# A decoder trunk on one core: where the low parts of the leading weights are made at the hand-over between two products

## The chip, the cores and the metric

The kernel runs on one core of one Trainium2 chip. What is measured is the device time of one execution in microseconds (us); lower is better. Engines are named as the profile names them: PE is TensorE, with its weight loads as PEld; DVE is VectorE, ACT is ScalarE, POOL is GpSimd, SP is SyncE, which here only issues transfers.

## The reference

A decoder trunk of two layers on a sequence of 512 positions, model width 1024, all in float32. Each layer has a token mixer and a dense SwiGLU network, each between two RMS norms:

```python
normed = rms_norm(h, mix_norm_pre[layer])
mixed = retention_mixer(...) if layer < N_A_LAYERS else nsa_mixer(..., shared)
h = h + rms_norm(mixed, mix_norm_post[layer])
normed = rms_norm(h, ffn_norm_pre[layer])
h = h + rms_norm(swiglu_ffn(normed, ffn_w_in[layer], ffn_w_out[layer]), ffn_norm_post[layer])
```

The first mixer is a retention, the second a sparse attention over keys and values that are computed once between the layers (`nsa_shared_kv`). `rms_norm` multiplies by the reciprocal root of the mean square over the 1024 features and by a gain. So every product is followed by two norms in a row: one of the product, which is added to the stream `h`, and one of `h`, whose result is the input of the next product.

## The kernel before

Every float32 product is made of three products of the short type float32r. Each operand is split into a high part (a ScalarE copy that rounds, L208 and L237) and a low part (the difference of the operand and its high part, L209 and L238), and `mm3` (L243 to L245) adds high by high, high by low and low by high. Weights stream in by chunks of 128x1024 (512 KB): `raw_weights` (L225) issues the transfer from SP into one of three raw buffers, ScalarE makes the high part, another engine the low part; a raw buffer is free for the next transfer when both have read it. Kept parts live in an arena `R` of 60 slots of 128x512, from which `weights(keep=True)` takes two pairs.

The change lies in `out_stage`, which ends a mixer or a network. It computes an output product row-wise, positions on the partitions: four blocks `b` of 128 positions, two halves `c` of 512 features, one PSUM bank for each. The last five chunks of half 1 are kept (`kept`), so that blocks 0 and 1 can be finished first, and blocks 2 and 3 after them. In the third of the three stages spoken of here, a sixth chunk (`defer`) is treated so as well. While TensorE computes blocks 2 and 3, `norm(..., 0)` works on blocks 0 and 1: a reciprocal root by three Newton steps on 128x2 numbers on VectorE (`rsqrt`, L266 to L273), the addition to `h` (L352, VectorE), the squares of `h` with their sum (L353, ScalarE), a second reciprocal root (L354 and `rsqrt`), and the scaled rows (L356 on ScalarE for the one block, L357 on VectorE for the other). Then `turn(t, p, kp, ...)` transposes two slabs of 128 features of a pair `p` of blocks on TensorE (L366, four transposes), and ScalarE and VectorE split them into the high and low parts of the next product's input (L369, L370). `lead` fetches and splits the first six weight chunks of the next product, "the leading weights", and `prods(j, k, cs)` multiplies chunk `j` by slab `k` for half of the positions, 256 columns. Three chunks are multiplied as slabs appear, three after all slabs. Then `norm(..., 1)` and `turn(..., 1, ...)` do the same for blocks 2 and 3, whose products `rest` makes later.

Order. PE and DVE follow the written order inside `manual_schedule`; ACT, POOL and SP instructions there are placed by the framework's scheduler. `pool_lo` is true inside this part, so the low parts of the leading weights go to GpSimd. There are three such stages: the retention's output (leads the network of layer 0), that network's output (leads the shared keys and values, and also copies the turned slabs, L376), and the attention's output (leads the network of layer 1). The fourth call of `out_stage` returns early and has no lead.

Of the kernel before, what the change touches and what calls it, by code (L numbers as in the profile page):

```python
# [10 lines left out]
F32 = mybir.dt.float32  # L11
# [3 lines left out]
OP = mybir.AluOpType  # L15
# [19 lines left out]
NR, NF = 60, 27  # L35
RAW, SPL = 3, 2
TAIL = 10

G_MIXPRE0, G_MIXPOST0, G_FFNPRE0, G_FFNPOST0, G_KV, G_MIXPRE1, G_MIXPOST1, G_FFNPRE1, G_FFNPOST1 = range(9)

# [127 lines left out]
class Trunk:  # L168
    def __init__(self, ctx, tc, a):
        self.tc, self.nc, self.a = tc, tc.nc, a  # L170
        pool = lambda name, **k: ctx.enter_context(tc.tile_pool(name=name, bufs=1, **k))
        self.cst = pool("cst")
        self.wp = pool("wp")
        arena = pool("arena")
        self.R = Arena(arena, NR, F32R, "r")
        self.F = Arena(arena, NF, F32, "f")
        self.banks = pool("ps", space=bass.MemoryType.PSUM).tile([P, 8, S], F32, name="banks")
        self.dram = pool("dram", space=bass.MemoryType.DRAM)
        self.n = 0
        self.pool_lo = False  # L180
        nc = self.nc
        self.ones = self.cst.tile([P, P], F32, name="ones")
        nc.gpsimd.memset(self.ones, 1.0)
        self.ident = self.cst.tile([P, P], F32, name="ident")
        nc.gpsimd.dma_start(self.ident, a["ident"])
        self.gains = self.cst.tile([P, 9, KT], F32, name="gains")
        nc.sync.dma_start(self.gains, a["gains"])
# [40 lines left out]
    def weights(self, src, off, row, n, keep=False):  # L228
        raw = self.raw_weights(src, off, row, n)
        if keep:  # L230
            w = Pair(self.R.take(2), self.R.take(2))
            hi, lo = w.hi.ap, w.lo.ap
        else:
            hi = self.wp.tile([P, 1024], F32R, name=self.nm("whi"), tag="whi", bufs=SPL)
            lo = self.wp.tile([P, 1024], F32R, name=self.nm("wlo"), tag="wlo", bufs=SPL)
            w = Pair(hi, lo)
        self.nc.scalar.activation(hi[:, :n], raw[:, :n], AF.Copy)  # L237
        (self.nc.gpsimd if self.pool_lo else self.nc.vector).tensor_tensor(lo[:, :n], raw[:, :n], hi[:, :n].bitcast(F32), op=OP.subtract)  # L238
        return w

    def mm3(self, out, shi, slo, mhi, mlo, start, stop):
# [98 lines left out]
        for x in st["x"]:  # L340
            x.free()

    def norm(self, h, t, sq, pre, p):

        nc = self.nc
        bs = slice(2 * p, 2 * p + 2)
# [3 lines left out]
        for i in range(2):  # L350
            b = 2 * p + i
            nc.vector.scalar_tensor_tensor(h[b].ap, t[b].ap, r[:, i:i + 1], h[b].ap, op0=OP.mult, op1=OP.add)  # L352
            nc.scalar.activation(t[b].ap, h[b].ap, AF.Square, accum_out=s2[:, i:i + 1])  # L353
        nc.vector.tensor_scalar(m2, s2, 1.0 / D, EPS, op0=OP.mult, op1=OP.add)  # L354
        r2 = self.rsqrt(m2, 2, True)
        nc.scalar.activation(t[2 * p].ap, h[2 * p].ap, AF.Copy, scale=r2[:, 0:1])  # L356
# [21 lines left out]
    def out_stage(self, x, src, nk, gpost, gpre, get_h, lead, banks, late=None, begun=None, keep=None):  # L378
# [15 lines left out]
        def chunk(c, i, keep=False):  # L394
            return self.weights(src, c * P * nk * S + i * S, nk * S, 2 * S, keep)

        def mm(c, i, w, blocks):
            for kk in range(2):
                k, ws = i + kk, slice(kk * S, (kk + 1) * S)
                for b in blocks:  # L400
                    bs = slice(b * P, (b + 1) * P)
                    self.mm3(bank[c][b], x[k].hi[:, bs], x[k].lo[:, bs], w.hi[:, ws], w.lo[:, ws], k == 0, k == nk - 1)
# [52 lines left out]
        E = mybir.EngineType  # L455
        st = self.state()
        st["n"] = []
        self.pool_lo = True
        with self.tc.manual_schedule(engines={E.PE, E.DVE}):
            for b in range(2):  # L460
                for i in kept:
                    mm(1, i, kept[i], (b,))
                evac(1, b)
            self.norm(h, t, sq, pre[0], 0)
            if begun:
                mm(0, begun, defer, (2, 3))
                defer.free()
                for b in (2, 3):
                    evac(0, b)
                pre[1] = early(1)  # L470
            for i in kept:
                mm(1, i, kept[i], (2, 3))
                kept[i].free()
                free(i)
            for b in (2, 3):
                evac(1, b)
            row.free()
            order, ws, prods = lead(st, A + B[:2])
            for kp in range(KT // 2 + 1):
                if kp < KT // 2:  # L480
                    self.turn(t, 0, kp, bank[1][kp % 2], gpre, st, keep is not None)
                if kp:
                    for k in (2 * kp - 2, 2 * kp - 1):
                        for j in range(3):
                            prods(j, k, HALVES[0])
            for b in range(2):
                t[b].free()
            for j in range(3, len(order)):
                for k in range(KT):
                    prods(j, k, HALVES[0])  # L490
            self.norm(h, t, sq, pre[1], 1)
            for kp in range(KT // 2):
                self.turn(t, 1, kp, bank[1][2 + kp % 2], gpre, st, keep is not None)
            for b in (2, 3):
                t[b].free()
        if keep is not None:
            for b in range(NB):
                nc.scalar.dma_start(keep[b], h[b].ap)
                h[b].free()
        self.pool_lo = False  # L500

        def rest(j0):
            j = order.index(j0)
# [7 lines left out]

    def lead(self, x, src, tiles, banks, base=0):

        ws = [self.chunk(src, j, KT, 0, base=base, keep=True) for j in tiles]

        def prods(j, k, cs):
            ks = slice(k * P, (k + 1) * P)
            self.mm3(self.banks[:, banks[j], cs], ws[j].hi[:, ks], ws[j].lo[:, ks], x[k].hi[:, cs], x[k].lo[:, cs],
                     k == 0, k == KT - 1)
        return tiles, ws, prods  # L520

    def ffn_lead(self, l):
        def go(st, banks):
# [1099 lines left out]
```

## Time and profile before

| | us |
|---|---|
| median of 3 runs (lowest, highest) | 1513.77 (1512.81, 1514.18) |
| the profiled execution | 1516.28 |
| span of its instructions | 1514.5 |

The profile is of one execution. Its span runs from the first to the last instruction; the execution's own time is 1.8 us longer. A row of a timeline gives the start in the span, the duration, the engine, the line, the operation, what it writes and reads, and in brackets how long the engine stood idle before it and what ended that. A row ending in "x2" holds two instructions back to back. TensorE's products overlap: a 128x512 product is listed with 0.39 us, though the next one starts 0.227 us later. "PEclk" is the clock that TensorE was granted, as a share of 2.4 GHz; 0.50 is its other level, 1.2 GHz.

### The profile page before, as it was taken

The page shows a single profiled execution, that of the slowest core. Times are in us where ns is not written, and L with a number is a line of the kernel's source. Part 1 is how long each engine was busy: PE and PEld are TensorE (multiplying, and loading weights), DVE is VectorE, ACT ScalarE, POOL GpSimd, SP SyncE. Part 2 cuts the span into 40 slices and gives each one's busy share as a digit, 9 for nine tenths or more (in the row PEclk, how much of TensorE's full clock was granted, in tenths as well). Part 3 has the DMA queues.
Part 4 walks back from the last instruction along what each step waited for, and adds up shares of the span by engine and source line. Part 5 has one row for each costly group of instructions (what it writes and reads, how often), then busy time and mean ns, then how long its engine had stood idle before and what let it go on. Part 6 is the DMA issues. An engine that isn't in the chain of part 4 may idle for free.

```text
span 1514.5 us, 18688 instructions
## 1 busy us (share of the span) xinstructions
PE 1473.5 (97%) x7294; PEld 1242.8 (82%) x7294; DVE 741.1 (49%) x1297; ACT 599.3 (40%) x1048; POOL 294.2 (19%) x387
## 2 busy tenths in 40 slices
PE   8999999999989999999998999999989999999997
PEld 6888888888788888888877978888879888888886
DVE  7456464735553333332345646888755333333234
ACT  5333343333332222221335337889744222222131
POOL 2022121211300000000030737877440000000000
PEclk9999999999989999999998999999998999999999
DMA  5222232325312344332342341221240232332231
GB/s 205 83 78 84 78 97 77 98 80 174 125 57 84 122 130 137 114 104 97 111 148 89 112 159 61 87 84 50 89 134 30 69 97 95 110 95 95 97 123 56
DMA packets 47833, 151.87 MB, mean 100 GB/s; under 512 B 5744, under 2 KB 6384, under 8 KB 47744
## 3 DMA queue, kind: packets, MB, share of 16 engines
q1 hardware_dynamic: 46560, 147.47, 30.3%
q10 hardware_dynamic: 1152, 3.15, 0.5%
q8 instruction: 57, 0.93, 0.2%
q14 instruction: 32, 0.26, 0.1%
q0 software_dynamic: 32, 0.07, 0.0%
HBM read 141.22 MB, written 9.44 MB: 99 GB/s over the span
## 4 chain that ended last, share of the span: by engine, by line
PE 91%; DVE 5%; ACT 2%; issue 1%; DMA 1%; POOL 0%; SPq 0%; DVEq 0%; ACTq 0%
PE banks L244 27%; PE banks L243 27%; PE banks L245 27%; PE banks L1470 2%; PE banks L1492 1%; PE banks L1404 1%; PE banks L1405 1%; PE banks L1491 1%; PE banks L983 1%; DVE t L270 1%; PE banks L366 1%; DVE u L271 1%; DVE y L266 0%; PE banks L1302 0%; DVE f L352 0%
## 5 line engine op out<-in xcount | busy, mean ns | idle before, releaser
L237 ACT ACTIVATE whi<-raw 128x1024 fp32r<-128x1024 f32 x165 | 174.7, 1059 | 514.9 <-PE banks L244 330.8
L243 PE MATMUL banks<-r,whi 128*128 128x512 f32 x920 | 361.4, 393 | 0.0
L245 PE MATMUL banks<-r,wlo 128*128 128x512 f32 x920 | 360.1, 391 | 0.0
L244 PE MATMUL banks<-r,whi 128*128 128x512 f32 x920 | 359.2, 390 | 0.0
L238 DVE TENSOR_TENSOR wlo<-raw,whi 128x1024 fp32r<-128x1024 f32 x165 | 206.0, 1249 | 296.3 <-ACT whi L237 290.2
L243 PE MATMUL banks<-r 128*128 128x256 f32 (+2 forms) x600 | 197.5, 338 | 7.7 <-ACT r L208 5.8
L244 PE MATMUL banks<-r 128*128 128x256 f32 (+2 forms) x600 | 201.2, 338 | 3.1 <-DVE r L370 2.5
L245 PEld LDWEIGHTS banks<-r,wlo 128*128 128x128 f32 x920 | 172.4, 187 | 37.5 <-DVE f L648 0.7
L244 PE MATMUL banks<-wlo,r 128*128 128x512 f32 x520 | 202.9, 390 | 0.0
L245 PE MATMUL banks<-whi,r 128*128 128x512 f32 x520 | 202.6, 390 | 0.0
L243 PEld LDWEIGHTS banks<-r,whi 128*128 128x128 f32 x920 | 172.5, 188 | 36.2 <-issue 1.6
L244 PEld LDWEIGHTS banks<-r,whi 128*128 128x128 f32 x920 | 172.5, 187 | 35.2 <-issue 0.5
L245 PE MATMUL banks<-r 128*128 128x256 f32 (+2 forms) x600 | 198.3, 334 | 0.0
L243 PE MATMUL banks<-whi,r 128*128 128x512 f32 x520 | 178.5, 390 | 0.0
L243 PEld LDWEIGHTS banks<-r 128*128 128x128 f32 x600 | 115.5, 196 | 20.4 <-ACT r L208 5.8
L244 PEld LDWEIGHTS banks<-r 128*128 128x128 f32 x600 | 117.6, 196 | 16.3 <-DVE r L370 5.5
L238 POOL TENSOR_TENSOR r<-raw,r 128x1024 fp32r<-128x1024 f32 x18 | 43.9, 2457 | 434.3 <-ACT r L237 421.7
L245 PEld LDWEIGHTS banks<-r 128*128 128x128 f32 x600 | 117.6, 196 | 10.0 <-DVE r L209 0.2
L245 PEld LDWEIGHTS banks<-whi,r 128*128 128x128 f32 x520 | 97.6, 188 | 20.3 <-issue 0.2
L244 PEld LDWEIGHTS banks<-wlo,r 128*128 128x128 f32 x520 | 97.7, 188 | 20.2 <-issue 0.2
L243 PEld LDWEIGHTS banks<-whi,r 128*128 128x128 f32 x520 | 97.7, 188 | 19.8
L545 DVE TENSOR_TENSOR f<-banks,f 128x512 f32<-128x512 f32 x44 | 30.4, 691 | 137.7 <-PE banks L245 133.6
(175 smaller groups left out, 1721.9 us busy)
## 6 DMA issues: line engine op xcount, KB each, us to landing
raw<-in_ffn_w_in_dram SPq DMA_DIRECT2D x88, 512.0 KB, 3.5
raw<-in_ffn_w_out_dram SPq DMA_DIRECT2D x44, 512.0 KB, 3.3
raw<-in_ret_w_g_dram SPq DMA_DIRECT2D x16, 512.0 KB, 3.5
raw<-in_ret_w_v_dram SPq DMA_DIRECT2D x16, 512.0 KB, 3.7
raw<-in_ret_w_out_dram SPq DMA_DIRECT2D x16, 512.0 KB, 3.8
f<-rows SPq DMA_DIRECT2D x32, 256.0 KB, 2.6
raw<-in_ret_w_qk_dram SPq DMA_DIRECT2D x12, 512.0 KB, 3.5
rows<-f SPq DMA_DIRECT2D x16, 320.0 KB, 4.4
```

Of the source, the lines that this page charges most:

```text
L237: self.nc.scalar.activation(hi[:, :n], raw[:, :n], AF.Copy)
L238: (self.nc.gpsimd if self.pool_lo else self.nc.vector).tensor_tensor(lo[:, :n], raw[:, :n], hi[:, :n].bitcast(F32), op=OP.subtract)
L243: t.matmul(out, shi, mhi, start=start, stop=False)
L244: t.matmul(out, shi, mlo, start=False, stop=False)
L245: t.matmul(out, slo, mhi, start=False, stop=stop)
L270: e.tensor_tensor(t, y, y, op=OP.mult)
L271: e.tensor_tensor(u, t, m, op=OP.mult)
L366: nc.tensor.transpose(bank[:, i * 256 + b * P:i * 256 + (b + 1) * P], t[2 * p + b][:, k * P:(k + 1) * P], self.ident)
L545: nc.vector.tensor_tensor(u.ap, pu, t.ap, op=OP.mult)
L983: nc.tensor.matmul(ph[:, :NG * NCMP], box["w1", which, m, c][:, j * P:(j + 1) * P], box["xv", which][:, c * 8 + j].rearrange("p g n -> p ( ...
L1404: nc.tensor.matmul(ps, qb, kh[:, ks, :w], start=True, stop=False)
L1470: nc.tensor.transpose(bank[2][:, c:c + P], probs[br][b][:, kb * P:(kb + 1) * P], self.ident)
```

## The change

`low` parts of leading weights are no longer made where the high part is made. `weights(keep=LATER)` returns a pair with a function `low`, which `out_stage` calls at written places, always on VectorE; `pool_lo` is gone. `lead` returns a function `more`, which fetches leading weights as long as the arena has two free pairs; it is called before the manual part, after `defer`, and after each kept chunk that blocks 2 and 3 have used. The places of the six low parts are: 0 after the evacuation of block 0; 1 inside the first norm, between the additions and the second reciprocal root; 2 and 3 before the last kept chunk's products; 4 after the second turn; 5 inside the second norm. The first four transposes (`turn(0, 0)`) stand between the first and the second half of the last kept chunk's products. The first norm is now written after the first two kept chunks of blocks 2 and 3, the second before the products of chunks 3 to 5, neither of which moves anything on TensorE, since a norm has no instruction there.

```diff
-        (self.nc.gpsimd if self.pool_lo else self.nc.vector).tensor_tensor(lo[:, :n], raw[:, :n], hi[:, :n].bitcast(F32), op=OP.subtract)
+
+        def low():
+            self.nc.vector.tensor_tensor(lo[:, :n], raw[:, :n], hi[:, :n].bitcast(F32), op=OP.subtract)
+        if keep == LATER:
+            w.low = low
+        else:
+            low()
         return w
...
-    def norm(self, h, t, sq, pre, p):
+    def norm(self, h, t, sq, pre, p, meanwhile):
...
             nc.scalar.activation(t[b].ap, h[b].ap, AF.Square, accum_out=s2[:, i:i + 1])
+        meanwhile()
         nc.vector.tensor_scalar(m2, s2, 1.0 / D, EPS, op0=OP.mult, op1=OP.add)
...
-        def mm(c, i, w, blocks):
+        def mm(c, i, w, blocks, inside=None):
             for kk in range(2):
+                if kk and inside:
+                    inside()
...
-        self.pool_lo = True
+        order, more, ws, prods = lead(st, A + B[:2])
+        low = lambda j: ws[j].low()
+        turn = lambda p, kp: self.turn(t, p, kp, bank[1][2 * p + kp % 2], gpre, st, keep is not None)
+        more()
         with self.tc.manual_schedule(engines={E.PE, E.DVE}):
             for b in range(2):
                 for i in kept:
                     mm(1, i, kept[i], (b,))
                 evac(1, b)
-            self.norm(h, t, sq, pre[0], 0)
+                if b == 0:
+                    low(0)
             if begun:
                 mm(0, begun, defer, (2, 3))
                 defer.free()
+                more()
+
+            def second(i, inside=None):
+                mm(1, i, kept[i], (2, 3), inside)
+                kept[i].free()
+                free(i)
+                more()
+            tail = sorted(kept)
+            for i in tail[:2]:
+                second(i)
+            self.norm(h, t, sq, pre[0], 0, lambda: low(1))
+            if begun:
                 for b in (2, 3):
                     evac(0, b)
                 pre[1] = early(1)
-            for i in kept:
-                mm(1, i, kept[i], (2, 3))
-                kept[i].free()
-                free(i)
+            for i in tail[2:-1]:
+                second(i)
+            low(2)
+            low(3)
+            second(tail[-1], lambda: turn(0, 0))
             for b in (2, 3):
                 evac(1, b)
             row.free()
-            order, ws, prods = lead(st, A + B[:2])
-            for kp in range(KT // 2 + 1):
+            for kp in range(1, KT // 2 + 1):
                 if kp < KT // 2:
-                    self.turn(t, 0, kp, bank[1][kp % 2], gpre, st, keep is not None)
-                if kp:
-                    for k in (2 * kp - 2, 2 * kp - 1):
-                        for j in range(3):
-                            prods(j, k, HALVES[0])
+                    turn(0, kp)
+                if kp == 1:
+                    low(4)
+                for k in (2 * kp - 2, 2 * kp - 1):
+                    for j in range(3):
+                        prods(j, k, HALVES[0])
             for b in range(2):
                 t[b].free()
+            self.norm(h, t, sq, pre[1], 1, lambda: low(5))
             for j in range(3, len(order)):
...
-            self.norm(h, t, sq, pre[1], 1)
...
     def lead(self, x, src, tiles, banks, base=0):
-        ws = [self.chunk(src, j, KT, 0, base=base, keep=True) for j in tiles]
+        ws = []
+
+        def more():
+            while len(ws) < len(tiles) and self.R.fits((2, 2)):
+                ws.append(self.chunk(src, tiles[len(ws)], KT, 0, base=base, keep=LATER))
```

What this makes of the queues is shown in the first stage, the retention's output, and the other two are alike except where said. The line numbers of the changed kernel differ: L238 has become L240, L243 to L245 are L249 to L251, L352 is L358, L353 is L359, L356 is L363, L357 is L364, L366 is L373, L369 is L376, L370 is L377, L408 and L409 are L417 and L418.

On VectorE, from the addition of the first norm to the split of the turned slabs, it was so before (`wlo` are the low parts of the chunks that follow the leading ones):

```order
L352 SCALAR_TENSOR_TENSOR f<-f,y_2798 128x1024 x2
L354 TENSOR_SCALAR m_2778<-s_2777 128x2
...
L357 TENSOR_SCALAR f<-f,y_2825 128x1024
L238 TENSOR_TENSOR wlo_3355<-raw_3352,whi_3354 128x1024
L409 TENSOR_TENSOR f<-banks,f 128x512 x2
L370 SCALAR_TENSOR_TENSOR r<-banks,gains,r 128x256
L238 TENSOR_TENSOR wlo_3386<-raw_3383,whi_3385 128x1024
L370 SCALAR_TENSOR_TENSOR r<-banks,gains,r 128x256 x7
```

and it is so now (raw_2792, raw_2795, raw_2810 and raw_2881 are leading chunks 1 to 4):

```order
L358 SCALAR_TENSOR_TENSOR f<-f,y_2835 128x1024 x2
L240 TENSOR_TENSOR r<-raw_2792,r 128x1024
L361 TENSOR_SCALAR m_2815<-s_2814 128x2
...
L364 TENSOR_SCALAR f<-f,y_2863 128x1024
L240 TENSOR_TENSOR r<-raw_2795,r 128x1024
L240 TENSOR_TENSOR r<-raw_2810,r 128x1024
L377 SCALAR_TENSOR_TENSOR r<-banks,gains,r 128x256 x2
L418 TENSOR_TENSOR f<-banks,f 128x512 x2
...
L240 TENSOR_TENSOR wlo_3355<-raw_3352,whi_3354 128x1024
L377 SCALAR_TENSOR_TENSOR r<-banks,gains,r 128x256
L240 TENSOR_TENSOR r<-raw_2881,r 128x1024
L377 SCALAR_TENSOR_TENSOR r<-banks,gains,r 128x256 x3
```

Four low parts have come in among the norm's and the slabs' instructions (parts 0 and 5 lie outside this piece), and the first turned block's low halves (L377 x2) stand ahead of the evacuation of blocks 2 and 3 (L418).

On ScalarE, around the scaled rows on which the first transpose waits (L356, L363), it was so before, with raw_2907, raw_2911 and raw_2915 the leading chunks 3 to 5:

```order
L353 ACTIVATE f,s_2777<-f 128x1024
L237 ACTIVATE r<-raw_2907 128x1024
...
L237 ACTIVATE r<-raw_2911 128x1024
L237 ACTIVATE r<-raw_2915 128x1024
L356 ACTIVATE f<-f,y_2825 128x1024
L237 ACTIVATE whi_3354<-raw_3352 128x1024
L408 ACTIVATE f,sq_2289<-banks 128x512 x2
L369 ACTIVATE r<-banks,gains 128x256 x2
L237 ACTIVATE whi_3385<-raw_3383 128x1024
```

and it is so now, with raw_2810, raw_2881 and raw_2884 the leading chunks 3 to 5:

```order
L237 ACTIVATE r<-raw_2810 128x1024
L359 ACTIVATE f,s_2814<-f 128x1024
L237 ACTIVATE r<-raw_2881 128x1024
L363 ACTIVATE f<-f,y_2863 128x1024
L376 ACTIVATE r<-banks,gains 128x256
L417 ACTIVATE f,sq_2289<-banks 128x512 x2
L376 ACTIVATE r<-banks,gains 128x256 x2
L237 ACTIVATE r<-raw_2884 128x1024
L237 ACTIVATE whi_3354<-raw_3352 128x1024
L376 ACTIVATE r<-banks,gains 128x256 x4
L237 ACTIVATE whi_3385<-raw_3383 128x1024
L376 ACTIVATE r<-banks,gains 128x256
```

One copy of a leading chunk still stands ahead of the scaled rows, that of chunk 4, and two copies (chunk 5 and the first chunk after the lead) stand between the third and the fourth slab's high parts. In the second stage chunk 4's copy stands behind the scaled rows instead.

On TensorE, at the end of the row products, the eight transposes of the first two turns stood together before:

```order
L243 MATMUL banks<-r 128x512
L244 MATMUL banks<-r 128x512
L245 MATMUL banks<-r 128x512
L366 MATMUL banks<-ident,f 128x128 x8
L243 MATMUL banks<-r 128x256
L244 MATMUL banks<-r 128x256
```

and now six row products stand between them:

```order
L251 MATMUL banks<-r 128x512
L373 MATMUL banks<-ident,f 128x128 x4
L249 MATMUL banks<-r 128x512
L250 MATMUL banks<-r 128x512
...
L251 MATMUL banks<-r 128x512
L373 MATMUL banks<-ident,f 128x128 x4
L249 MATMUL banks<-r 128x256
```

Nothing else on TensorE has moved. The order of SP's transfers is the same; what each waits for is not: a raw buffer is now freed by a low part on VectorE instead of one on GpSimd.

## Rows read from the trace of the kernel before

**Rows 1.** The page: busy time of the engines, share of the span, instructions.

```profile
PE 1473.5 (97%) x7294; PEld 1242.8 (82%) x7294; DVE 741.1 (49%) x1297; ACT 599.3 (40%) x1048; POOL 294.2 (19%) x387
```

**Rows 2.** TensorE's waits in stages 2 and 3: waiter, releaser, us, times, longest.

```profile
PE banks L366 <- ACT f L356: 5.4, 1, 5.4
...
PE banks L366 <- ACT f L356: 4.4, 1, 4.4
```

**Rows 3.** Sums by stretch, one for each stage: length, engines' busy us, PEclk, DMA.

```profile
413.30:445.80 32.50, 23.57 (x162) 22.74 (x162) 20.99 (x52) 12.03 (x21) 4.95 (x3) 0.79 0.25 81
...
792.70:824.00 31.30, 24.40 (x161) 23.25 (x161) 18.92 (x54) 14.59 (x29) 4.82 (x3) 0.78 0.35 119
1131.00:1159.70 28.70, 23.02 (x161) 22.13 (x161) 19.12 (x52) 11.23 (x20) 1.75 (x1) 0.82 0.24 75
```

**Rows 4.** Timeline of TensorE, stage 1: first and fifth group of transposes.

```profile
421.13 1.97 PE L366 MATMUL banks<-ident,f 128*128 128x128 f32 x8 [7.68 <-ACT f L356]
...
445.76 1.04 PE L366 MATMUL banks<-ident,f 128*128 128x128 f32 x8
```

**Rows 5.** Sums by stretch: two parts of stage 1's stretch, low and full clock.

```profile
431.00:446.00 15.00, 15.00 (x128) 15.00 (x127) 8.23 (x30) 4.71 (x8) 0.00 (x0) 1.00 0.00 2
...
417.40:431.00 13.60, 8.63 (x37) 7.94 (x38) 8.70 (x19) 6.51 (x13) 0.85 (x1) 0.50 0.44 151
```

**Rows 6.** Timeline of VectorE, stage 1: the first norm.

```profile
401.21 0.15 DVE L348 SCALAR_TENSOR_TENSOR ms<-sq,pre 128x2 f32<-128x2 f32 x1
...
402.77 2.35 DVE L270 TENSOR_TENSOR t<-y 128x2 f32<-128x2 f32 x1
...
407.69 2.48 DVE L352 SCALAR_TENSOR_TENSOR f<-f,y 128x1024 f32<-128x1024 f32 x2
412.25 1.43 DVE L354 TENSOR_SCALAR m<-s 128x2 f32<-128x2 f32 x1 [2.07 <-ACT f L353]
413.71 2.26 DVE L266 TENSOR_SCALAR y<-m 128x2 int32<-128x2 int32 x1
...
419.86 0.75 DVE L357 TENSOR_SCALAR f<-f,y 128x1024 f32<-128x1024 f32 x1
```

**Rows 7.** Timeline of GpSimd in the same stretch: low parts of leading weights.

```profile
402.70 4.74 POOL L238 TENSOR_TENSOR r<-raw,r 128x1024 fp32r<-128x1024 f32 x2 [12.52 <-PE banks L245]
411.25 7.00 POOL L238 TENSOR_TENSOR r<-raw,r 128x1024 fp32r<-128x1024 f32 x3 [3.81 <-ACT r L237]
```

**Rows 8.** Timelines of VectorE and ScalarE, stage 1: the second norm.

```profile
434.94 0.15 DVE L348 SCALAR_TENSOR_TENSOR ms<-sq,pre 128x2 f32<-128x2 f32 x1
...
437.08 2.48 DVE L352 SCALAR_TENSOR_TENSOR f<-f,y 128x1024 f32<-128x1024 f32 x2
440.78 0.17 DVE L354 TENSOR_SCALAR m<-s 128x2 f32<-128x2 f32 x1 [1.22 <-ACT f L353]
...
443.02 1.16 ACT L356 ACTIVATE f<-f,y 128x1024 f32<-128x1024 f32 x1 [2.27 <-DVE y L273]
```

**Rows 9.** A chunk's steps: its transfer (KB, median us to landing), high part, low part.

```profile
raw<-in_ffn_w_in_dram SPq DMA_DIRECT2D x88, 512.0 KB, 3.5
...
410.13 1.04 ACT L237 ACTIVATE r<-raw 128x1024 fp32r<-128x1024 f32 x1
...
422.05 1.23 DVE L238 TENSOR_TENSOR wlo<-raw,whi 128x1024 fp32r<-128x1024 f32 x1 [1.44 <-ACT whi L237]
```

**Rows 10.** A slab's low part behind its high part, stage 1, VectorE.

```profile
427.43 0.48 DVE L370 SCALAR_TENSOR_TENSOR r<-banks,gains,r 128x256 fp32r<-128x256 f32 x1 [0.54 <-ACT r L369]
```

**Rows 11.** TensorE at two waits of 1.07 us, and the clock after each.

```profile
896.92 1.77 PE L1126 MATMUL banks<-f 128*128 128x64 f32 x14 [1.07 <-DVE f L1033]
...
898.70:902.00 3.30, 3.30 (x9) 1.54 (x8) 0.41 (x1) 2.71 (x7) 3.18 (x3) 0.50 0.54 159
...
1089.62 0.66 PE L1470 MATMUL banks<-ident,f 128*128 128x128 f32 x4 [1.07 <-DVE r L1481]
...
1087.50:1090.80 3.30, 2.23 (x15) 1.73 (x14) 3.00 (x4) 1.98 (x4) 0.00 (x0) 1.00 0.86 322
```

More of the change, by code (lines that the diff above doesn't have):

```diff
@@ L37 @@
 TAIL = 10
+LATER = 2
 G_MIXPRE0, G_MIXPOST0, G_FFNPRE0, G_FFNPOST0, G_KV, G_MIXPRE1, G_MIXPOST1, G_FFNPRE1, G_FFNPOST1 = range(9)
@@ L179, in __init__ @@
         self.n = 0
-        self.pool_lo = False
         nc = self.nc
@@ L490, in out_stage @@
                     prods(j, k, HALVES[0])
-            self.norm(h, t, sq, pre[1], 1)
             for kp in range(KT // 2):
-                self.turn(t, 1, kp, bank[1][2 + kp % 2], gpre, st, keep is not None)
+                turn(1, kp)
             for b in (2, 3):
@@ L499, in out_stage @@
                 h[b].free()
-        self.pool_lo = False
         def rest(j0):
@@ L519, in prods @@
                      k == 0, k == KT - 1)
-        return tiles, ws, prods
+        return tiles, more, ws, prods
     def ffn_lead(self, l):
```

## The prediction, made before the change was run

> **What bounds the kernel now.** I read the page's busy times first: TensorE works 1473.5 of 1514.5 us [rows 1], so a change gains only where TensorE waits or runs at its lower clock. The list of TensorE's waits shows one large wait at each of three places, always of the first transpose (L366) for the scaled rows at the end of the first norm (L356): 7.68 us in stage 1 [rows 4], 5.4 and 4.4 in stages 2 and 3 [rows 2]. The sums by stretch then show what each hand-over costs in all. Each stretch of [rows 3] runs from the last row product to the fifth group of transposes, where the second pair of blocks begins: 32.5, 31.3 and 28.7 us, together 92.5. TensorE has the same to do in each: 16 transposes and 144 products of 256 columns. At the full clock 128 such instructions take 15.00 us [rows 5], 0.117 us each, so the 160 take 18.8 us, and three stretches 56.3. The other 36.2 us are waits and half clock: in stage 1 the granted clock is 0.50, that is 1.2 GHz, from 417.4 to 431.0 [rows 5]; it fell while TensorE stood idle until 421.13 [rows 4].
>
> Why TensorE waits is read from VectorE's timeline, stage 1. The first norm begins at 401.21. Its 128x2 steps take some 0.15 us, but 402.77 and the next take 2.3 us each, 412.25 takes 1.43, 413.71 and one more 2.25 each [rows 6]. GpSimd makes two low parts from 402.70 in 4.74 us and three from 411.25 in 7.00 [rows 7], and the long steps end where these end: 402.77 + 2.35 = 405.12, and 402.70 + 4.74 / 2 = 405.07. In the second norm, with GpSimd idle, the first root takes 437.08 - 434.94 = 2.14 us and the second, to the start of the scaling, 443.02 - 440.78 = 2.24 [rows 8]; in the first norm they take 6.48 and 7.61 [rows 6].
>
> **The change, part by part (stage 1, then the others).**
>
> *No low parts on GpSimd.* The first norm loses 4.3 + 5.4 = 9.7 us. The additions (L352) start at 401.21 + 2.14 = 403.35 and the scaling could start at 410.2, where it started at about 419.9. The row products end at 413.3 (start of the stretch in [rows 3]), so the wait of 7.68 is gone, as are those of 5.4 and 4.4, which are shorter than the same 9.7.
>
> *Eighteen low parts more on VectorE*, 1.23 us each [rows 9], 22 us, six to a stage. Part 0 stands between the evacuations of two blocks; part 1 at 405.9, after the additions, where VectorE now waits 2.07 us for the squares [rows 6]; part 5 in the same place of the second norm (1.22 idle there, [rows 8]). These three I cost at nothing; without that idle time each would delay its norm by up to 1.23. Parts 2 and 3 follow L357: 410.9 to 413.3, before VectorE has a slab to split. Part 4 counts below.
>
> *First turn before the last six row products.* These take 6 x 0.227 = 1.36 us and cover the split of the first slab (0.54 + 0.48, [rows 10]), on which TensorE would else wait.
>
> *What is late next.* A raw buffer is now free only when VectorE has come to the low part, and the transfers of the later leading chunks and their copies on ScalarE follow from that. Chunk 4's transfer starts with the end of part 1, 407.1, lands 3.5 us later at 410.6, and its copy (1.04) stands ahead of the scaling: 411.7, scaled rows (1.16) at 412.8. TensorE comes to the transposes at 413.3 - 1.36 = 411.9: it waits 0.9. Chunk 5's transfer starts after part 2 at 412.1 and lands at 415.6, that of the first chunk after the lead after part 3 at 413.3, landing 416.9; both copies stand ahead of the fourth slab's high part, 418.5, and VectorE makes that chunk's low part (419.2) ahead of the slab's, 419.7. TensorE, from 412.8 on with 12 transposes, six row products and 27 slab products, is there at 418.6 and waits 1.1. The second chunk after the lead gets its buffer at 419.2, lands at 422.7, is copied by 423.8, split by 425.0, and the eighth slab's low part follows at 425.5; TensorE is there at 424.4 and waits 1.1. With fractions at the slabs between, some 4 us a stage; stage 2, where chunk 4's copy comes after the scaling, pays for the copies of L376 instead. Bounds: nothing, if every transfer is early, and 6, twice the sum, if each transfer takes 5 to 6 us instead of 3.5. I take 4, from the median transfer.
>
> *Second norm.* It starts at 425.5 and takes 443.02 + 1.16 - 434.94 = 9.2 us: 434.7. TensorE has 9 + 72 products from 425.5, to 435.0. Just covered; one microsecond more on VectorE would show as a wait here.
>
> *Sum.* A stretch takes 18.8 + 4 = 22.8 us, three 68.4, against 92.5: 24 us less. *The clock.* Each stretch now has waits of about 1 us. Rows show both outcomes: after one of 1.07 us (and products of 64 columns) the clock was at 0.50 at 898.7, after another of 1.07 it stayed at 1.00 [rows 11]. If it fell for as long as in [rows 5], with 8.6 us of work at half speed, each stretch would lose 4.3, 13 in all; nothing is the other end. I allow 3, about a quarter, since one of the two waits kept it. So 21 us less: the profiled execution's 1516.28 becomes 1495.3. It lies 2.5 above the median of the runs, 1513.77, which I carry over: **1493 us**, 1.4% faster.
>
> **The rivals.**
>
> *The clock falls in all three stretches.* For it: the first of the two waits in [rows 11], and three waits a stretch now. Against it: the stretches that fell had waits of 4.4 to 7.7 first. With half clock for 13.6 us all of it worked, a stretch takes 18.8 + 6.8 + 0.9 = 26.5 (a slower TensorE no longer meets the two later waits), 79.5 in all, 13 less than now: 1501. The Trainium skill speaks for this one: "TensorE: Matmul & The Clock Gate", section "A second HAM failure mode: psum-queue depth-cycling", tells of a kernel whose TensorE idles briefly but often between groups of products, and whose clock went back and forth between its levels. By that rule the result would be this rival's 1501 and not 1493; of the waits in [rows 11] one agrees and one does not.
>
> *Transfers too late (slower).* Place: the three raw buffers. Each stretch now has three waits in a row for a transfer that starts only after a low part. The gain is 24 over nine such waits, 2.7 each, so it decides at a landing time of 3.5 + 2.7 = 6.2 us; at 8 us, 4.5 more in each of nine, 40 less the 24, the kernel would take 1530. For it: it is a real chain, absent before. Against: a median of 3.5 [rows 9] and little else on the queues there (DMA at 0.25 to 0.35 of its time [rows 3]).
>
> *The long steps are not GpSimd's doing.* If they came from ScalarE's wide copies beside them, the norm would stay as long, and parts 2 and 3 (2.46) would come on top after it, less the 1.2 that the first turn's place saves: about 1.3 a stage, 1518. Against it: the ends that coincide [rows 6, 7].
>
> **How the numbers follow.** Forecast, 1486 to 1498: 0.82. Clock rival, about 1501: 0.12. Late transfers: 0.03. Not GpSimd's doing: 0.03. The low end, 1487, is 6 under the forecast: no clock loss and waits of 3 instead of 4. The high end, 1501, is the clock rival. With no waits at all it would be 1513.8 - 36.2 = 1477.6, which I leave out, since the chain above is long. A measurement of this kernel tells 0.2%, about 3 us, from no change. The first two cases are faster by more than that, 0.94; for no change I keep 0.02 of the last two, and 0.04 for slower.
>
> **What would show it.** Right: no VectorE step of 128x2 over 0.5 us in the three stretches; no low part of a chunk on GpSimd; stretches of 22 to 24 us; the wait for the scaled rows about 1 us, and at the fourth and the eighth slab about 1 us each, ended by VectorE's low part. Wrong: half clock for over 10 us in a stretch; ScalarE waiting over 5 us for a chunk; the fifth group of transposes waiting for the second norm.

## The result, and the profile after

The changed kernel takes **1492.09 us** (median of 4 runs, 1491.42 to 1493.78); the kernel before, run beside it, 1513.97 (1512.81 to 1514.18). The ratio is 0.9859, with a 95% interval of 0.9842 to 0.9876: 21.9 us or 1.4% faster. Forecast were 1493, with 1487 to 1501 as the range (the low end stands as 1486 where the chances are given). The profiled execution took 1491.88 with a span of 1490.1; that is 24.4 less than the profiled one before, which lay 2.5 above its median.

The page's busy times, which answer to [rows 1]:

```profile
PE 1463.3 (98%) x7294; PEld 1233.0 (83%) x7294; DVE 736.2 (49%) x1315; ACT 599.1 (40%) x1048; POOL 250.1 (17%) x369
```

TensorE has as many instructions as before. Eighteen have gone from GpSimd (387 to 369) to VectorE (1297 to 1315), and VectorE is busy 4.9 us less all the same: its held steps are gone.

Sums by stretch, one for each stage, from the first turned block (with the wait in front of it) to the fifth group of transposes. The columns are those of [rows 3]:

```profile
411.83:435.48 23.65, 21.59 (x166) 20.45 (x167) 17.14 (x42) 11.52 (x21) 0.00 (x0) 1.00 0.42 134
780.92:807.01 26.09, 23.13 (x168) 21.86 (x166) 17.56 (x45) 14.14 (x29) 0.00 (x0) 0.93 0.47 162
1110.93:1135.98 25.05, 21.88 (x166) 20.57 (x167) 18.32 (x44) 11.76 (x21) 0.00 (x0) 1.00 0.39 126
```

These stretches begin earlier in TensorE's work than those of [rows 3], by the six row products that now follow the first turn, 1.36 us. Without them they take 22.3, 24.7 and 23.7 us, together 70.7 against 92.5. That is 21.8 of the 24.4 us by which the span is shorter; 1.7 more is the 3.4 us of half clock at 898.7 [rows 11], which this execution does not have. The last 0.9 was not followed up.

The timeline of VectorE in stage 1, the first norm and what follows:

```profile
400.95 0.15 DVE L354 SCALAR_TENSOR_TENSOR ms<-sq,pre 128x2 f32<-128x2 f32 x1
...
403.10 2.48 DVE L358 SCALAR_TENSOR_TENSOR f<-f,y 128x1024 f32<-128x1024 f32 x2
405.50 1.22 DVE L240 TENSOR_TENSOR r<-raw,r 128x1024 fp32r<-128x1024 f32 x1
407.66 0.17 DVE L361 TENSOR_SCALAR m<-s 128x2 f32<-128x2 f32 x1 [0.94 <-ACT f L359]
...
409.83 0.75 DVE L364 TENSOR_SCALAR f<-f,y 128x1024 f32<-128x1024 f32 x1
410.50 2.35 DVE L240 TENSOR_TENSOR r<-raw,r 128x1024 fp32r<-128x1024 f32 x2
...
418.29 1.23 DVE L240 TENSOR_TENSOR wlo<-raw,whi 128x1024 fp32r<-128x1024 f32 x1 [0.65 <-ACT whi L237]
...
425.66 0.15 DVE L354 SCALAR_TENSOR_TENSOR ms<-sq,pre 128x2 f32<-128x2 f32 x1
```

From the norm's first step to its scaling on VectorE (L364) it takes 8.9 us; before it was 419.86 - 401.21 = 18.65 [rows 6]. No step on 128x2 numbers takes more than 0.17. The low part at 405.50 lies in the time in which VectorE waits for the squares, and 0.94 of that wait is still left behind it.

ScalarE's timeline around the scaled rows (L363) of the first norm, and that of the second:

```profile
410.23 1.06 ACT L237 ACTIVATE r<-raw 128x1024 fp32r<-128x1024 f32 x1 [2.61 <-DMA raw<-in_ffn_w_in_dram]
411.20 1.13 ACT L363 ACTIVATE f<-f,y 128x1024 f32<-128x1024 f32 x1
...
433.74 1.15 ACT L363 ACTIVATE f<-f,y 128x1024 f32<-128x1024 f32 x1 [2.26 <-DVE y L279]
```

The factors of the first scaling are there at 409.8, but a chunk's copy stands ahead of it and waits for its transfer. That is what is left of the wait of [rows 4]. TensorE's timeline, where it waits in stage 1, with the products just before, and the fifth transposes:

```profile
411.44 0.39 PE L251 MATMUL banks<-r 128*128 128x512 f32 x1
412.39 0.65 PE L373 MATMUL banks<-ident,f 128*128 128x128 f32 x4 [0.56 <-ACT f L363]
...
418.64 0.28 PE L251 MATMUL banks<-r 128*128 128x256 f32 x1
419.04 0.38 PE L249 MATMUL banks<-r 128*128 128x256 f32 x1
419.96 0.38 PE L250 MATMUL banks<-r 128*128 128x256 f32 x1 [0.54 <-DVE r L377]
...
424.71 0.28 PE L249 MATMUL banks<-r 128*128 128x256 f32 x1
425.80 0.38 PE L250 MATMUL banks<-r 128*128 128x256 f32 x1 [0.81 <-DVE r L377]
...
435.48 1.03 PE L373 MATMUL banks<-ident,f 128*128 128x128 f32 x8
```

The wait in brackets counts from the listed end of the product before. The next product could have started earlier, 0.227 us after a product of 512 columns and 0.12 after one of 256. Counted so, from start to start, the transposes come 412.39 - 411.44 - 0.23 = 0.72 us late, the fourth slab 419.96 - 418.64 - 0.24 = 1.08, and the eighth 425.80 - 424.71 - 0.12 = 0.97.

In stage 2 the first transposes do not wait, and in stage 3 they wait 0.67, instead of 5.4 and 4.4 [rows 2]. Stage 3 is else like stage 1: 0.86 and 0.54 are listed at the fourth slab and 0.91 at the eighth. What TensorE meets in stage 2 is a slab whose high part (L376) stands on ScalarE behind a copy that waits for its transfer:

```profile
789.54 0.38 PE L249 MATMUL banks<-r 128*128 128x256 f32 x1 [1.56 <-ACT r L376]
790.90 0.39 PE L250 MATMUL banks<-r 128*128 128x256 f32 x1 [0.98 <-DVE r L377]
```

```profile
788.07 1.06 ACT L1195 ACTIVATE whi<-raw 128x1024 fp32r<-128x1024 f32 x1 [1.87 <-DMA raw<-in_kv_w_n_dram]
```

This transfer was issued at 782.20, as soon as part 3 had freed its buffer, and took 5.8 us to land, where the median of [rows 9] is 3.5. Behind this pair of waits the clock fell, the only time in the three stretches, for 3.4 us; the sum over 3.3 us of them:

```profile
791.30:794.60 3.30, 3.30 (x17) 3.30 (x17) 2.04 (x4) 1.31 (x4) 0.00 (x0) 0.50 0.78 256
```

### The profile page after: what moved, and what is told of

Its sections match the earlier page's. It is cut to its first block, busy times and chain, and to the rows that moved or that the text cites. A ratio compares the mean times of both kernels' runs of the same rounds, so it can differ in the third digit from the quotient of the medians.

```text
span 1490.1 us, 18671 instructions
## 1 busy us (share of the span) xinstructions
PE 1463.3 (98%) x7294; PEld 1233.0 (83%) x7294; DVE 736.2 (49%) x1315; ACT 599.1 (40%) x1048; POOL 250.1 (17%) x369
## 4 chain that ended last, share of the span: by engine, by line
PE 91%; DVE 4%; DMA 2%; ACT 2%; issue 1%; POOL 0%; SPq 0%; DVEq 0%; ACTq 0%
PE banks L250 27%; PE banks L249 27%; PE banks L251 27%; PE banks L1500 2%; PE banks L1522 1%; PE banks L1434 1%; PE banks L1435 1%; PE banks L1521 1%; DMA raw<-in_ffn_w_in_dram 1%; PE banks L1013 1%; DVE r L240 1%; PE banks L1332 1%; DVE r L1511 0%; DMA raw<-in_kv_w_n_dram 0%; PE banks L373 0%
## 5 line engine op out<-in xcount | busy, mean ns | idle before, releaser
L249 PE MATMUL banks<-r,whi 128*128 128x512 f32 x920 | 360.8, 392 | 0.0
L251 PE MATMUL banks<-r,wlo 128*128 128x512 f32 x920 | 359.6, 391 | 0.0
L240 DVE TENSOR_TENSOR wlo<-raw,whi 128x1024 fp32r<-128x1024 f32 x165 | 206.0, 1249 | 299.3 <-ACT whi L237 293.1
L249 PE MATMUL banks<-r 128*128 128x256 f32 (+2 forms) x600 | 194.5, 333 | 8.9 <-ACT r L208 5.9
L251 PEld LDWEIGHTS banks<-r,wlo 128*128 128x128 f32 x920 | 172.2, 187 | 37.4 <-DVE f L678 0.7
L250 PE MATMUL banks<-r 128*128 128x256 f32 (+2 forms) x600 | 198.5, 334 | 4.6 <-DVE r L377 3.8
L251 PE MATMUL banks<-whi,r 128*128 128x512 f32 x520 | 202.6, 390 | 0.0
L249 PEld LDWEIGHTS banks<-r,whi 128*128 128x128 f32 x920 | 172.3, 187 | 35.5 <-issue 0.9
L251 PE MATMUL banks<-r 128*128 128x256 f32 (+2 forms) x600 | 195.5, 329 | 0.0
L249 PE MATMUL banks<-whi,r 128*128 128x512 f32 x520 | 178.5, 390 | 0.0
L249 PEld LDWEIGHTS banks<-r 128*128 128x128 f32 x600 | 112.3, 191 | 20.9 <-ACT r L208 5.9
L250 PEld LDWEIGHTS banks<-r 128*128 128x128 f32 x600 | 114.5, 191 | 18.1 <-DVE r L377 7.4
L251 PEld LDWEIGHTS banks<-r 128*128 128x128 f32 x600 | 114.5, 191 | 10.2 <-DVE r L209 0.5
L251 PEld LDWEIGHTS banks<-whi,r 128*128 128x128 f32 x520 | 97.7, 188 | 20.3 <-issue 0.2
L249 PEld LDWEIGHTS banks<-whi,r 128*128 128x128 f32 x520 | 97.7, 188 | 19.9
L575 DVE TENSOR_TENSOR f<-banks,f 128x512 f32<-128x512 f32 x44 | 30.4, 692 | 137.7 <-PE banks L251 133.5
L949 POOL TENSOR_TENSOR r<-f,r 64x512 fp32r<-64x512 f32 x8 | 10.8, 1350 | 493.1 <-ACT r L942 492.8
```

Source lines behind the costliest of these rows:

```text
L240: self.nc.vector.tensor_tensor(lo[:, :n], raw[:, :n], hi[:, :n].bitcast(F32), op=OP.subtract)
L249: t.matmul(out, shi, mhi, start=start, stop=False)
L250: t.matmul(out, shi, mlo, start=False, stop=False)
L251: t.matmul(out, slo, mhi, start=False, stop=stop)
L575: nc.vector.tensor_tensor(u.ap, pu, t.ap, op=OP.mult)
```

## The experiments

The theory: GpSimd's low parts held VectorE's small steps (theory G below), and the written places keep the low parts from delaying something else. Rivals: the first turn's place brings the gain; taking GpSimd out is enough, wherever the low parts then stand; the places are enough, on any engine. The kernel before was run beside each of them (1512.6 to 1514.2).

### The places alone: the low parts stay on GpSimd

```diff
-            self.nc.vector.tensor_tensor(lo[:, :n], raw[:, :n], hi[:, :n].bitcast(F32), op=OP.subtract)
+            (self.nc.gpsimd if keep == LATER else self.nc.vector).tensor_tensor(lo[:, :n], raw[:, :n], hi[:, :n].bitcast(F32), op=OP.subtract)
```

> The changed kernel with the six low parts of each stage made by GpSimd again, all else as changed (early fetch, first turn inside, their place in the text). Theory G (the low parts on GpSimd hold VectorE's norm steps, and that is the loss): steps of 128x2 of 1.4 to 2.4 us are back in the first norm, the wait for the scaled rows is 4 to 8 us again in each stage, and the time is within 5 us of the kernel before, 1509 to 1519. Rival P (the early fetch and the first turn's place make the gain): it stays at 1492 to 1497.

Measured: 1512.46 us (1511.85 to 1513.47), 0.9989 of before (0.9980 to 0.9998). VectorE's and GpSimd's timelines and TensorE's first transposes in stage 1:

```profile
403.03 2.35 DVE L276 TENSOR_TENSOR t<-y 128x2 f32<-128x2 f32 x1
405.41 2.31 DVE L277 TENSOR_TENSOR u<-t,m 128x2 f32<-128x2 f32 x1
```

```profile
402.96 4.74 POOL L240 TENSOR_TENSOR r<-raw,r 128x1024 fp32r<-128x1024 f32 x2 [12.16 <-PE banks L251]
```

```profile
421.35 1.11 PE L373 MATMUL banks<-ident,f 128*128 128x128 f32 x4 [9.01 <-ACT f L363]
```

The long steps are back beside GpSimd's work, and nearly the whole gain is gone. TensorE waits 9.01 instead of 7.68 [rows 4], since the first turn now stands 1.36 us earlier; in stages 2 and 3 it waits 6.77 and 5.84. The places and the early fetch alone bring some 2 us, less than 0.2%.

### The first turn alone, in the kernel before

```diff
+            last = max(kept)
             for i in kept:
-                mm(1, i, kept[i], (2, 3))
+                mm(1, i, kept[i], (2, 3), (lambda: self.turn(t, 0, 0, bank[1][0], gpre, st, keep is not None)) if i == last else None)
...
-                if kp < KT // 2:
+                if 0 < kp < KT // 2:
```

> The kernel before with one part of the change: the first turn's four transposes stand before the last six row products. Theory G: the scaled rows come at the same time as before, so TensorE only waits earlier, and the six products run after the wait instead of ahead of it; what is saved is the split of the first slab, some 1.2 us a stage: 1510 to 1515. Rival P: a good part of the 22 us, below 1505.

Measured: 1511.93 us (1511.06 to 1514.95), 0.9985 (0.9976 to 0.9994). The first transposes:

```profile
422.86 1.11 PE L366 MATMUL banks<-ident,f 128*128 128x128 f32 x4 [9.01 <-ACT f L356]
```

The order of TensorE's instructions is not what was in the way.

### GpSimd out, without the places: six low parts in a row on VectorE, in the kernel before

```diff
-        self.pool_lo = True
+        self.pool_lo = False
```

> The kernel before with the low parts of the leading weights on VectorE, all six in a row where the text fetches them, after the evacuation of blocks 2 and 3 and before the first slab's split. Theory G: no long 128x2 step is left and the first norm is 9 us shorter, but the six low parts, 7 us of VectorE, and the transfers that wait for them stand ahead of the first slab's low part; TensorE waits for that instead, 8 to 12 us a stage where it waited 4 to 8 for the norm: 1512 to 1526, no gain. Rival V (it is enough to leave GpSimd, the places do not matter): 1492 to 1498.

Measured: 1522.99 us (1521.47 to 1523.68), 1.0056 (1.0042 to 1.0069): slower than before. VectorE's timeline in stage 1, and TensorE's wait:

```profile
409.31 0.75 DVE L357 TENSOR_SCALAR f<-f,y 128x1024 f32<-128x1024 f32 x1
...
414.90 3.48 DVE L238 TENSOR_TENSOR r<-raw,r 128x1024 fp32r<-128x1024 f32 x3
...
424.39 1.23 DVE L238 TENSOR_TENSOR r<-raw,r 128x1024 fp32r<-128x1024 f32 x1 [0.17 <-ACT r L237]
```

```profile
426.06 0.58 PE L244 MATMUL banks<-r 128*128 128x256 f32 x1 [11.00 <-DVE r L370]
```

The norm is as quick as in the changed kernel, its scaling on VectorE at 409.31, and the first transposes do not wait for it. But the first slab's split now stands behind six low parts. The last three wait for copies on ScalarE, which wait for their transfers (4.66 us for the first of them), and TensorE waits 11.0, 11.3 and 11.3 us in the three stages. So neither half of the change gains without the other: GpSimd out costs some 9 us, the places or the turn alone gain some 2, and both together gain 22. This version also lacks the early fetch of the changed kernel; how much of its loss is due to that, and how much to the low parts standing in a row, was not tried.

### One GpSimd operation put back beside the first norm of the changed kernel

```diff
+            extra = self.F.take(2)
+            nc.gpsimd.tensor_tensor(extra.ap, t[0].ap, t[1].ap, op=OP.add)
+            extra.free()
...
             self.norm(h, t, sq, pre[0], 0, lambda: low(1))
```

It is an addition that nothing reads, once in each stage.

> The changed kernel with one more GpSimd instruction in each stage, an addition of two 128x1024 tiles whose result nothing reads, which can start with the first norm. Theory G: GpSimd takes about 2.4 us for it, one 128x2 step of VectorE beside it takes about 2.3 us instead of 0.16, the scaled rows come 2.3 us later, and since TensorE waits for them already the time grows by 2 to 3 us a stage: 1498 to 1502 (1504 if the clock falls in the longer wait). Rival S (the long steps came from ScalarE's wide copies): no change, 1490 to 1494.

Measured: 1500.45 us (1498.49 to 1501.81), 0.9904 (0.9889 to 0.9919), 8.4 more than the changed kernel's 1492.09, which was measured beside other runs; by the ratios to the kernel before, 0.9904 and 0.9859, it is 6.8. GpSimd and VectorE in stage 1, and TensorE's first transposes:

```profile
401.73 2.40 POOL L479 TENSOR_TENSOR f<-f 128x1024 f32<-128x1024 f32 x1 [49.73 <-DVE ms L354]
```

```profile
401.75 2.40 DVE L272 TENSOR_SCALAR y<-ms 128x2 int32<-128x2 int32 x1
```

```profile
416.15 1.12 PE L373 MATMUL banks<-ident,f 128*128 128x128 f32 x4 [3.71 <-ACT f L363]
```

One step of 0.17 us takes 2.40, as long as the operation beside it, and ends with it. In stages 2 and 3 one step is held as well, for 2.40 and 2.32 us. The kernels differ in nothing but this addition, so the hold is shown by itself. The three holds lengthen the steps by 6.6 us; TensorE's waits for the scaled rows come to 8.1 in all, against 1.2. The clock also fell in stages 1 and 3 of this execution, to 0.88 and 0.94 over the stretch.

### The first turn behind the row products, in the changed kernel

```diff
-            second(tail[-1], lambda: turn(0, 0))
+            second(tail[-1])
...
+            turn(0, 0)
```

> The changed kernel with the first turn back behind the last row products. Theory G: the scaled rows are ready at about the end of the row products, so no wait is left ahead of the transposes, but TensorE then waits for the split of the first slabs, 1 to 2 us more in each stage where the change waits 0.6: 1493 to 1497. Rival P: the place of the first turn carries the gain, over 1500.

Measured: 1494.58 us (1494.01 to 1495.36), 0.9874 (0.9858 to 0.9889); the changed kernel beside it 1491.56 (1490.82 to 1492.16), 0.9852 (0.9834 to 0.9870), as expected of it:

> The changed kernel as it is, on the same chip as the other runs: 1491 to 1494, so that differences of 1 to 2 us between them can be read.

TensorE's timeline at the first slab, stage 1:

```profile
414.41 0.38 PE L249 MATMUL banks<-r 128*128 128x256 f32 x1 [0.27 <-ACT r L376]
415.17 0.39 PE L250 MATMUL banks<-r 128*128 128x256 f32 x1 [0.38 <-DVE r L377]
```

The split of the first slab is now waited for, in two pieces. The place of the first turn is worth 3.0 us in the changed kernel. That this is 1.0 a stage, as the cover of 0.54 + 0.48 in the prediction has it [rows 10], is not shown: between the two profiled executions the stretches, counted alike, differ by 2.9, 0.1 and 1.0 us, and in stages 1 and 3 the clock fell (0.94 and 0.93 over the stretch, at most 1.6 and 1.8 us lost), where it stayed at 1.00 in the changed kernel. Without the clock some 0.5 us is left in three stages. Whether the waits for the first slab made the clock fall stays open.

### A fourth raw buffer

The copy ahead of the scaling waits for a transfer, and that for a raw buffer. With a fourth buffer it should start earlier. Its memory is taken from the other arena, so that was also made smaller alone.

```diff
-NR, NF = 60, 27
-RAW, SPL = 3, 2
+NR, NF = 60, 25
+RAW, SPL = 4, 2
```

> The changed kernel with four raw buffers for weight chunks instead of three (and 25 slots of the float32 arena instead of 27, for the space). If the waits that are left come from chunks whose transfer begins only after a low part has freed a buffer, ScalarE no longer waits for a transfer in the stages, the waits at the fourth and eighth slab shrink from 0.5 to 0.8 us towards nothing: 3 to 8 us less than the changed kernel, 1484 to 1489. If they come from the work itself on VectorE and ScalarE (low parts, copies), no change within 2 us.

> The changed kernel with 25 slots of the float32 arena instead of 27 and three raw buffers: what the other run pays for its space. The same as the changed kernel within 1.5 us, 1490.5 to 1493.5; more would mean that the float32 slots hold something up in the attention.

Measured: 1492.22 us with four buffers (1488.83 to 1493.61; 0.9854, 0.9835 to 0.9874), and 1493.49 with the smaller arena alone (1492.63 to 1493.84; 0.9865, 0.9850 to 0.9880). The expected gain did not come. The waits at the eighth slab are gone, as expected (0.89 and 0.78 in stages 1 and 3 of the changed kernel beside it), but others are longer, and the listed waits of the three stages come to 8.9 us, against 7.9. ScalarE with four buffers, stage 1:

```profile
403.51 1.06 ACT L237 ACTIVATE r<-raw 128x1024 fp32r<-128x1024 f32 x1 [0.30 <-PE banks L251]
...
410.23 1.06 ACT L237 ACTIVATE r<-raw 128x1024 fp32r<-128x1024 f32 x1 [2.63 <-DMA raw<-in_ffn_w_in_dram]
411.20 1.13 ACT L363 ACTIVATE f<-f,y 128x1024 f32<-128x1024 f32 x1
```

One copy more is made early, at 403.51, and the framework's scheduler has moved the next chunk's copy up behind it: it stands ahead of the scaling, waits for its own transfer, and the scaling starts at 411.20 as with three buffers. So a buffer more did not move the scaling: a copy that waits stood ahead of it again.

### ScalarE's order by hand, the scaling ahead of the copy

```diff
-        self.nc.scalar.activation(hi[:, :n], raw[:, :n], AF.Copy)
+        def high():
+            self.nc.scalar.activation(hi[:, :n], raw[:, :n], AF.Copy)
+        w.high = high
+        if keep != LATEST:
+            high()
...
-        with self.tc.manual_schedule(engines={E.PE, E.DVE}):
+        with self.tc.manual_schedule(engines={E.PE, E.DVE, E.Activation}):
...
             for i in tail[2:-1]:
                 second(i)
+            ws[4].high()
...
                 if kp == 1:
                     low(4)
+                    ws[5].high()
```

`LATEST` marks leading chunks 4 and 5.

> ScalarE's order is written by hand here, with chunk 4's high part behind the scaling of the first norm and chunk 5's behind the second turn. Theory (the rest of the first wait is ScalarE's queue: the scaling stands behind a copy that waits for its transfer, whatever the number of buffers): the scaling starts with its factors, at about 409.9 instead of 411.20 in stage 1, the waits of the first transposes (0.56 in stage 1, 0.67 in stage 3) are below 0.2, and the kernel takes 1 to 2 us less than the changed one, 1490 to 1491. Rival (the wait moves on to the next slab, whose chunk now comes later): waits at the first transposes gone, waits for VectorE's low parts longer by as much, 1491.5 to 1493.

> The changed kernel beside it, on the same chip: 1491 to 1493.

Measured: 1504.72 us (1503.18 to 1505.55), 0.9938 (0.9923 to 0.9953); the changed kernel beside it 1493.48 (1491.32 to 1494.02), 0.9860 (0.9844 to 0.9877). It is a miss of both expectations, by over 11 us. ScalarE's timeline in stage 1 (L363 are the squares here, L367 the scaling, L238 the copies, L380 and L381 the parts of a slab):

```profile
406.13 1.06 ACT L238 ACTIVATE r<-raw 128x1024 fp32r<-128x1024 f32 x1 [0.71 <-PE banks L255]
407.10 1.04 ACT L363 ACTIVATE f<-f 128x1024 f32<-128x1024 f32 x1
...
411.53 1.16 ACT L367 ACTIVATE f<-f,y 128x1024 f32<-128x1024 f32 x1 [2.26 <-DVE y L283]
412.60 1.05 ACT L238 ACTIVATE r<-raw 128x1024 fp32r<-128x1024 f32 x1
...
418.88 1.06 ACT L238 ACTIVATE whi<-raw 128x1024 fp32r<-128x1024 f32 x1 [1.96 <-DMA raw<-in_ffn_w_in_dram]
419.84 0.46 ACT L380 ACTIVATE r<-banks,gains 128x256 fp32r<-128x256 f32 x1
```

The scaling now starts when its factors are there, and the first transposes wait in no stage; so far the theory holds. But the scaling starts at 411.53, not at 409.9 as expected: by hand all of ScalarE's work stands in written order, and a leading chunk's copy, which waits for TensorE (406.13), now stands ahead of the norm's squares. From its first step to its scaling on VectorE the norm takes 9.5 us instead of 8.9, and it begins 1.1 us later. Parts 2 and 3 end later with it, at 414.49 instead of 412.85, and so the transfer that needs part 3's buffer lands later: its copy starts at 418.88 instead of 417.20. It stands ahead of the fourth slab's high part, as it did in the changed kernel. TensorE in stage 1, and the sums of the three stretches, cut as above:

```profile
420.35 0.38 PE L253 MATMUL banks<-r 128*128 128x256 f32 x1 [1.39 <-ACT r L380]
421.64 0.50 PE L254 MATMUL banks<-r 128*128 128x256 f32 x1 [0.91 <-DVE r L381]
```

```profile
412.60:437.64 25.04, 22.74 (x169) 21.89 (x168) 18.10 (x43) 11.82 (x22) 0.00 (x0) 0.93 0.43 127
783.21:813.58 30.37, 25.08 (x167) 23.52 (x167) 18.18 (x45) 14.32 (x29) 0.00 (x0) 0.89 0.43 139
1120.98:1149.65 28.67, 24.39 (x167) 23.13 (x167) 19.83 (x46) 12.84 (x25) 0.00 (x0) 0.88 0.38 111
```

The three take 84.1 us instead of 74.8. The listed waits come to 11.9 us, 4 more than in the changed kernel. One of 1.78 us in stage 3 is for the first slab's split. On VectorE that stands behind an evacuation of blocks 2 and 3, whose part on ScalarE now comes behind the scaling (L421, at 1120.83 and 1121.40); the scheduler had put it far ahead of the scaling (L417, at 1100.82 and 1102.41). And the clock falls in each stretch: at half clock TensorE loses at most 0.07 x 25.0 + 0.11 x 30.4 + 0.12 x 28.7 = 8.5 us, against 0.07 x 26.1 = 1.8. Of the 13.7 us by which this span is longer, 9.3 lie here. Of the rest 0.8 lies ahead of stage 1's stretch and 3.5 between stages 2 and 3; it was not followed up. A version with the scaling alone moved and the rest of the scheduler's order kept was not tried. No kernel here beats the changed one.

## Why the prediction was right, point by point

**The norm.** Forecast: 9.7 us lost from the first norm, the factors there at 410.2. Measured: 409.83, 8.9 us after the norm's first step instead of 18.65, so 9.8 us lost. The rival that the long steps are not GpSimd's doing fell twice, with the low parts put back on GpSimd and with a single addition there.

**Parts at no cost.** Parts 1 to 3 lie where the prediction put them (405.50, and 410.50 to 412.85); behind part 1 there are 0.94 us to spare. Part 5 ends at 431.43, when the squares end too (431.48), so it just fits.

**What is late next.** This step was the least certain, and it held in its order: chunk 4's copy ahead of the scaling, then the fourth and the eighth slab. Its sizes were near in stage 1. Counted from start to start, as the prediction counted, TensorE is late by 0.72 for 0.9, 1.08 for 1.1 and 0.97 for 1.1. Chunk 4's copy started at 410.23, not at 410.6, and the scaling at 411.20, not 411.7. Stage 1 is 22.3 - 18.8 = 3.5 us above TensorE's own work, for the 4 forecast; the three places make 2.8 of it, and the rest lies in the fractions between. Stage 2 went otherwise: no wait at the scaled rows or at the eighth slab, but listed ones of 0.38, 1.56 and 0.98. The first is for the copies that the prediction named (L376, now L383). The others are at the fourth slab, behind the copy of the first chunk after the lead, a place that the prediction had named; its transfer landed in 5.8 us, near the 5 to 6 of the upper bound, not in 3.5. Summed up, the three stretches lost 70.7 - 56.3 = 14.4 us, of which at most 1.8 is the clock; forecast were 12 for waits and 3 for the clock. These two errors are small and of opposite sign, and that they nearly cancel is luck: of two more profiled executions of the changed kernel one shows no fall of the clock in the three stretches, the other one fall.

**First turn.** Its cover was put at 1.02 us a stage; taken away, it costs 3.0 us in three. The sum fits, but not the mechanism as far as the traces show it: most of the difference between the profiled executions is the clock, and stage 2 differs by 0.1 us only.

**Second norm.** Forecast "just covered", rows at 434.7 and TensorE there at 435.0. Measured: the scaling ends at 433.74 + 1.15 = 434.89, and the fifth transposes start at 435.48 with no wait.

**The signs named.** None of those for "wrong" came. Of those for "right", two held only in part: stage 2's stretch took 24.7 us, above the 22 to 24 named, and of the waits at the fourth slab those in stages 2 and 3 were ended first by ScalarE's high part and only then by VectorE's low part.

**The rivals.** Transfers too late: ScalarE's waits for a chunk shown above are 2.61 and 1.87 us, and the longest in the three stages is 2.72, where this case asked for over 5. A transfer still lands in 3.5 us at the median [rows 9], the slow one of stage 2 in 5.8. The clock: it fell in one of three stretches, for 3.4 us, where the prediction allowed 3 us of loss and the rival 13. The argument against it, that long waits came before each fall, did not hold: here two of 1.56 and 0.98 were enough. The Trainium skill, "TensorE: Matmul & The Clock Gate", section "A second HAM failure mode: psum-queue depth-cycling", describes a clock that goes back and forth where TensorE idles briefly but often. The changed kernel agrees only in stage 2 (0.93; 1.00 in the others). The version with ScalarE's order by hand agrees in every stretch (0.93, 0.89, 0.88), and it takes 1504.7, where this rival was given 1501; but 4 us more of listed waits are part of that, too. So the rival was the right one to price. What decided against it in the changed kernel is not shown.

## What to carry to other kernels

Look for small steps on VectorE that last as long as an operation on GpSimd and end with it; such work is better done by VectorE itself, but at places where it waits anyway, since the same work put in a row in front of something urgent made this kernel 9 us slower, although the hold was gone. A wait for a transfer is paid by whatever stands behind it on the same engine: see what the copy stands ahead of before buying another buffer. An order by hand here took in all of the engine's instructions: what the scheduler had put right came back as waits.

## What the runs showed of the hardware

A single GpSimd addition of 2.40 us held a VectorE step of 128x2 numbers with one operand for all of its own length (2.40 for 0.17). Three such holds cost the kernel 6.8 us by the ratios and 8.4 by the medians. The Trainium skill, "SBUF — State Buffer", section "🔬 SBUF: two separate sides", tells of a pair of ports that GpSimd and some kinds of VectorE instruction share, which one of them holds for a whole instruction while the other stands still. The trace agrees: the addition starts at 401.73, the step at 401.75, and both last 2.40 us.

The clock did not follow from a single wait's length. In the changed kernel it stayed at 1.00 through the stretch of stage 1 with waits of 0.56, 0.54 and 0.81 us, and fell behind two of 1.56 and 0.98 close together. With the first turn behind the row products it fell in stage 1 behind two of 0.96 and 0.91; in the kernel before, of two waits of 1.07, one was followed by half clock and one was not [rows 11].
